# Two-layer decoder step: one row distance of 384 columns for all normed activations, other places for weights, staging tiles and slots

## The chip, the cores and the metric

The kernel runs on one core of a Trainium2 chip. The metric is the device time of one execution in microseconds. Three runs of the kernel before gave 2852.44, 2856.76 and 2860.83 us; the median is 2856.76. One more execution was taken by the hardware profiler and took 2856.44 us.

## The reference

One inference step of a decoder with two layers over T = 1104 tokens: 64 of eight sample requests, 16 meta tokens and 1024 of a prompt. The width is 1024, all values are fp32.

```python
for l in range(DEPTH):
    if l < N_A_LAYERS:
        a, (C, n, m) = mlstm_mixer(rmsnorm(h, norm_a), C0, n0, m0, lead, w_in_a, b_ig_a, b_fg_a, mh_norm_a, w_out_a)
        h = h + a
    else:
        h = h + fox_mixer(rmsnorm(h, norm_b), shared, attend, w_qo_b, q_norm_b, w_out_b)
    h = h + swiglu(rmsnorm(h, norm_ffn[l]), w_gate_up[l], w_down[l])
    if l == N_A_LAYERS - 1:
        shared = shared_kv(h, norm_kv, w_kvf, b_fg_b, k_norm_b)
y = rmsnorm(h, norm_final)
```

The first mixer is a gated linear recurrence. Its input and forget gates are what the change touches:

```python
li = softcap(gi + b_ig)                  # softcap(x) = 15 tanh(x / 15)
lf = log_sigmoid(softcap(gf + b_fg))
h, state = mlstm_sequence(q, k, v, li, lf, state0, lead)
out = (rmsnorm(h, mh_g) * sigmoid(og)) @ w_out
```

The second mixer is softmax attention with forget gates over keys and values that are projected once (`shared_kv`), for the samples also over cached pages.

## The kernel before

**Layout.** Activations lie with the features on the partitions: 8 rows of 128 features, and the tokens along a row. The tokens are cut in three slabs, of 336, 384 and 384 columns in phase A (the first mixer, `TSA`) and of 368 columns each in everything after it (`TS`). An fp32 product is made of three products of a fast 32-bit type: high by high, high by low, low by high (`mm3`, L269 to L274). So each weight and each normed activation is split in two tiles: ACT casts the high part (L334) and DVE takes the difference (L335). The normed activations are the tiles x0h, x0l, x1h, x1l, x2h, x2l of `new_x` (L354 and following), one pair for each slab, with 8 rows of n columns. Before the change a row begins right behind the one ahead of it, so that the distance from row to row is n columns: 336, 384 or 368.

**Two kinds of matmul read them.** In the token-major kind x is the stationary operand, 128 tokens of it, and 256 columns of weights move past it: the V, output gate and gate projections of phase A, and the K, V and q projections after the first layer (outputs named tmps). In the feature-major kind a block of weights is stationary and a whole slab of x moves: the q/k projections of phase A (mmA), the output projections (pops), the gate of the second mixer (bps) and gate/up in the feed-forward networks (L1540).

**Order.** TensorE (PE), the DMA queue of SyncE (SP) and part of DVE run in the order in which the code is written; the others are ordered by a scheduler, and the memory by pools: a tile that is put where another one was waits for the last use of that one. The stages by time, in microseconds from the start of the span: load and norm to 55; phase A with the recurrence 55 to 435; first output projection 444 to 545; first feed-forward to 1260; K, V and q projections to 1605; attention to 2020; second output projection to 2115; second feed-forward to 2850.

**The gates** (`rec_prep`, L964 and following). The biases are loaded on POOL's DMA queue into gbias (L970, L971), the start states into m (L973). DVE adds the bias (L1014), ACT takes the tanh (L1015), DVE scales (L1016) and copies the forget half (lf_tm, L1018), from which a chain on DVE and ACT makes the log of the sigmoid. PE transposes gates and then lf_tm (rps, L1030). Just ahead of this, `cache_prep` makes the running sums of the cached forget values: cs is stored to csE by eight DMAs of POOL (L959, 256 KB each) from the pool that lies where the rows' pool (`rp`) comes next. POOL also sets two selection tiles, selP and selS. Before the change gbias and m are in the pool of phase A (`kp`).

**First output projection** (in `mlp`, L510 and following). SP loads a block of 128 columns of w_out_a (L535) into a raw tile: woraw or one of two slots in turn; ACT and DVE split it into wo. The gate values ogc are loaded by POOL from ogD (L900), where phase A has stored them from staging tiles (stg, copied from PSUM by ACT at L859, stored by POOL at L860), and go through a sigmoid on ACT (L901). The last heads of the recurrence are gated and transposed (ghps, L1477) between the units of the projection (pops). Before the change woraw and wo lie where the staging tiles were.

**The rest that the change touches.** The slots are ten areas of the right side that hold weights in the output projections and feed-forwards. nq are tiles for the squares of the residual (L407 to L412), nr one for a norm. hr tiles of the hidden values of the feed-forward are put by `cut` over the memory of x (L1646).

Of the kernel before, what the change touches and what calls it, by code (L numbers as in the profile page):

```python
# [7 lines left out]
F32 = mybir.dt.float32  # L8
F32R = mybir.dt.float32r
# [24 lines left out]
TT = [(a + P * x, min(a + P * x + P, b)) for a, b in TS for x in range(3)]  # L34
WX = [max(z[t][1] - z[t][0] for z in (TSA, TS)) for t in range(3)]
GRPA = [(0, 1, 2, 3), (4, 5, 6), (7, 8)]
# [219 lines left out]
class Net:  # L256
# [98 lines left out]
    def new_x(self, t):  # L355

        ts = self.parts[0]
        n = ts[t][1] - ts[t][0]
        self.X[t] = tuple(
            self.xp.tile([P, KT * WX[t]], F32R, name=self.uid(f"x{t}{s}"), tag=f"x{t}{s}")[:, : KT * n].rearrange(  # L360
                "p (k n) -> p k n", k=KT) for s in "hl"
        )
        return self.X[t]
# [36 lines left out]
    def add_sq(self, H, t, m, sp, x, late=KT - 1):  # L400

        nc = self.nc
        t0, t1 = TS[t]
        n = t1 - t0
        if x == 0:
            self.sums[t] = self.ns[:, t % 2, :n]
            nc.scalar.activation(self.sums[t], H[t][:, m], AF.Square)  # L407
            return
        sq = self.nq[:, x % 2, :n]
        nc.scalar.activation(sq, H[t][:, m], AF.Square)  # L410
        s = self.sums[t]
        (nc.vector if x >= late else nc.gpsimd).tensor_tensor(out=s, in0=s, in1=sq, op=ALU.add)  # L412
# [35 lines left out]
    def run(self):  # L448
        nc, tc, I, O, ctx = self.nc, self.tc, self.I, self.O, self.ctx
        self.consts()  # L450
        self.hD = self.dram.tile([P, KT, T], F32, name="hD")
        self.X = {}
        self.parts = TSA, TTA
# [3 lines left out]
        with ExitStack() as c1:  # L457
# [16 lines left out]
            slots = {0: both[:, 0], 1: both[:, 1]}  # L474
            for x, n in ((7, NP), (3, NP), (8, NP + 104), (2, NP)):
                slots[x] = wp.tile([P, n], F32R, name=self.uid("slot"))
            ws = self.attend_prompt(ys, slots, both, I["w_out_b"][0])
# [5 lines left out]
    def mlp(self, H, w, l, heads=None, cb=None, early=None):  # L483
# [8 lines left out]
        with self.pool(self.uid("nsp")) as sp, self.pool(self.uid("npp"), bufs=2, space=PSUM) as pn:  # L492
# [3 lines left out]
            def small(c, down=False):  # L496
                p = c.enter_context(self.pool(self.uid("small")))
                if down:
                    self.nq = p.tile([P, 2, SL], F32, name=self.uid("nq"))
                    self.ny = lambda nm: p.tile([P, 2 * SL if l else max(2 * SL, 3 * 256)], F32, name=nm, tag="ny", bufs=3)  # L500
                    return p
                self.nq = p.tile([P, 2, SL], F32, name=self.uid("nq"))

# [3 lines left out]
            if cb:  # L507
                cw = cb
                wp = cw.enter_context(self.pool(self.uid("slots"), side="right"))
                slots = {x: wp.tile([P, self.wmin], F32 if x < 2 else F32R, name=self.uid("slot")) for x in range(10)}  # L510
            else:
# [4 lines left out]
            with ExitStack() as c:  # L516
                small(c)
                fixed.enter_context(self.tc.manual_schedule(engines={E.PE}))
                gp = c.enter_context(self.pool(self.uid("gh")))
                wp = c.enter_context(self.pool(self.uid("wo")))  # L520
                pp = c.enter_context(self.pool(self.uid("po"), bufs=3, space=PSUM))
# [99 lines left out]
            with cw if not cb else ExitStack():  # L621
                def each(t, m):
                    if cb or t < 2 or m < KT - 2:
                        self.add_sq(H, t, m, sp, m)
                    else:
                        n = TS[t][1] - TS[t][0]
                        nc.scalar.activation(self.nq[:, m % 2, :n], H[t][:, m], AF.Square)
                        if m == KT - 1:
                            nc.vector.tensor_tensor(out=self.sums[t], in0=self.sums[t], in1=self.nq[:, 0, :n],
                                                    op=ALU.add)  # L630
# [332 lines left out]
def rec_prep(self, kp, gates, rp, pp):  # L963
# [3 lines left out]
    if True:  # L967

        bias = kp.tile([P, 16], F32, name="gbias")
        nc.gpsimd.dma_start(bias[:, :8], I["b_ig_a"][0].partition_broadcast(P))  # L970
        nc.gpsimd.dma_start(bias[:, 8:], I["b_fg_a"][0].partition_broadcast(P))  # L971
        m0 = kp.tile([HA, NB], F32, name="m0")
        nc.gpsimd.dma_start(m0, I["state_m"][0].rearrange("b h -> h b"))  # L973
# [516 lines left out]
def ffn(self, H, flat, l, weights, order, mix, small, each, after, end, early=None):  # L1490
# [9 lines left out]
    with self.pool(f"ffn{l}") as fp, self.pool(f"ffnp{l}", space=PSUM) as pp:  # L1500
# [19 lines left out]
        class Unit:  # L1520
# [96 lines left out]
            def tail(u):  # L1617
# [11 lines left out]

        cut = lambda ts, n: [tuple(y.rearrange("p k n -> p (k n)")[:, i * 2 * SL : i * 2 * SL + 2 * SL] for y in ts)  # L1630
                             for i in range(n)]
# [16 lines left out]
        def h_split(j):  # L1648
            if j < len(hseq):
                t, z, c = seq[hseq[j]]  # L1650
                x0, x1, x2 = (cut(self.X[y], n) for y, n in ((0, 3), (1, 4), (2, 4)))
                a = [y for x in (2, 1, 4) for y in cut(Tx[x], 2)] + x2
# [245 lines left out]
def final(self, H, flat, t, gr, sp, pools):  # L1898
# [5 lines left out]
    r = sp.tile([P, 3], F32, name=self.uid("fr"), tag="fr", bufs=2)  # L1904
    squares = [self.sums[t]] + ([self.nq[:, 1, : TS[t][1] - s0]] if t == 2 else [])
    tiles = [(x, i, min(TT[i][0], TS[t][1] - P), TT[i][1]) for x, i in enumerate(GRP[t])]
# [588 lines left out]
def attend_prompt(self, ys, slots, both, w):  # L2495
# [3 lines left out]
    with self.pool("ap", bufs=1) as sp, self.pool("ap2", bufs=2) as s2, self.pool("app", bufs=2, space=PSUM) as pp:  # L2499
# [53 lines left out]
        def load_v(hp, e):  # L2553
# [6 lines left out]
            for g in QG:  # L2560
# [5 lines left out]

        more = {7: 72}
        row = lambda hp, qb, z: s2.tile([P, NM + P * qb + more.get(qb, 0)], F32, name=f"s{hp}_{qb}_{z}",
                                        tag=f"s{qb}")[:, : NM + P * qb]

# [303 lines left out]
```

## Time and profile before

| | us |
|---|---|
| three runs | 2852.44, 2856.76, 2860.83 |
| profiled execution | 2856.44 |
| its span | 2854.7 |
| PE, weight loads (PEld) busy | 2784.9, 2662.2 |
| DVE, ACT, POOL busy | 1747.1, 1318.4, 1079.4 |
| mean granted clock of TensorE | 0.995 |
| moved by DMA | 400.08 MB, 140 GB/s |

The page names instructions by line, engine, operation and tiles, `out<-in`. In rows of groups there stand the count, the busy time, the mean of one in ns and the idle time of the engine ahead of them with what ended it. A row of waits reads: engine, what waited, what it waited for, us in total, times, longest. A row of the timeline reads: start, us, engine, line, what, and in brackets the idle time before. A row of windows gives for a stretch its length and for each engine the busy time and the count, then the granted clock. In a row of DMA issues the last number is the median from issue to landing.

### The profile page before, as it was taken

To read this page: it belongs to the slowest core of one execution; us is meant where nothing else is said; L and a number is where in the kernel's file an instruction comes from. 1 tells how busy PE (TensorE), PEld (TensorE's weight loads), DVE (VectorE), ACT (ScalarE), POOL (GpSimd) and SP (SyncE) were. 2 spreads that over 40 slices of the span, in tenths; PEclk is the share of its full clock that TensorE was granted. 3 is DMA by queue.
4 is the path that set the end of the run, shared out by engine and by line. 5 is a ranking of instruction groups with operands and counts; after the bars stand their busy time and mean duration, and the time that the engine had idled before them with its cause. 6 is when DMAs were issued, how large, how long until landed. Compare 5 with 4: busy or idle time off the path is not lost. (4 is left out here: it accounts for less than half of the span.)

```text
span 2854.7 us, 54143 instructions
## 1 busy us (share of the span) xinstructions
PE 2784.9 (98%) x20638; PEld 2662.2 (93%) x20638; DVE 1747.1 (61%) x3598; ACT 1318.4 (46%) x2629; POOL 1079.4 (38%) x1578
## 2 busy tenths in 40 slices
PE   8999998999999999999999999999999999999999
PEld 7997988989999999999999888777999999999998
DVE  6144564787777755553365543777468777875553
ACT  6222464445444534443344554877444454443432
POOL 3042323166666411117463201455307566631110
PEclk9999999999999999999999999999999999999999
DMA  6157655222222275544453686452412222236653
GB/s 213 30 133 168 166 154 161 77 79 79 90 79 79 83 276 198 199 152 148 133 165 121 213 298 223 152 172 88 155 53 88 79 79 88 77 110 241 212 190 105
DMA packets 314070, 400.08 MB, mean 140 GB/s; under 512 B 28998, under 2 KB 235826, under 8 KB 312786
## 3 DMA queue, kind: packets, MB, share of 16 engines
q1 hardware_dynamic: 277282, 277.66, 30.6%
q0 software_dynamic: 35776, 118.40, 12.8%
q8 instruction: 162, 2.65, 0.4%
q10 hardware_dynamic: 752, 0.57, 0.1%
q14 instruction: 98, 0.80, 0.1%
HBM read 299.78 MB, written 96.77 MB: 139 GB/s over the span
## 5 line engine op out<-in xcount | busy, mean ns | idle before, releaser
L335 DVE TENSOR_TENSOR slot<-slot,slot 128x1024 fp32r<-128x1024 f32 (+3 forms) x263 | 251.6, 959 | 117.1 <-ACT slot L334 112.5
L334 ACT CAST slot<-slot 128x1024 fp32r<-128x1024 f32 (+3 forms) x263 | 206.6, 788 | 226.6 <-PE dps L273 100.2
L1540 PE MATMUL m<-x0h,slot 128*128 128x368 f32 x640 | 178.4, 329 | 0.0
L1540 PE MATMUL m<-x1h,slot 128*128 128x368 f32 x640 | 174.8, 332 | 3.6 <-DVE ns L1517 1.9
L412 POOL TENSOR_TENSOR ns<-ns,nq 128x368 f32<-128x368 f32 x59 | 65.2, 1104 | 213.5 <-ACT nq L410 212.3
L1646 POOL DMA_DIRECT2D hr<-hT x60 | 32.4, 541 | 283.8 <-DVE T_2l L335 70.6
L1540 PE MATMUL m<-x2h,slot 128*128 128x368 f32 x480 | 132.3, 330 | 0.0
L114 POOL TENSOR_TENSOR slot<-vA 128x256 f32<-128x256 f32 x80 | 74.3, 939 | 151.5 <-DMA vA<-in_w_gate_up 147.7
L114 POOL TENSOR_TENSOR slot<-Ht 128x256 f32<-128x256 f32 x80 | 74.6, 943 | 150.5 <-DMA Ht<-in_w_gate_up 78.8
L335 DVE TENSOR_TENSOR slot<-Ht,slot 128x256 fp32r<-128x256 f32 (+3 forms) x101 | 90.0, 892 | 53.0 <-ACT slot L334 53.0
L335 DVE TENSOR_TENSOR slot<-vA,slot 128x256 fp32r<-128x256 f32 (+3 forms) x101 | 88.8, 881 | 54.5 <-ACT slot L334 54.5
L1540 PEld LDWEIGHTS m<-x1h,slot 128*128 128x128 f32 x640 | 115.8, 188 | 6.5 <-DVE ns L1517 2.5
L1540 PEld LDWEIGHTS m<-x0h,slot 128*128 128x128 f32 x640 | 116.0, 188 | 0.0
L1540 PE MATMUL m<-x1l,slot 128*128 128x368 f32 x320 | 105.5, 330 | 0.0
L1540 PE MATMUL m<-x0l,slot 128*128 128x368 f32 x320 | 105.2, 329 | 0.0
L2668 ACT ACTIVATE s<-s,nb 128x272 f32<-128x272 f32 (+7 forms) x126 | 98.9, 787 | 0.3 <-POOL nb L2659 0.3
L2703 ACT COPY th<-tp 128x768 f32<-128x768 f32 (+1 forms) x80 | 73.6, 921 | 45.9 <-PE tp L2695 24.9
L1540 PE MATMUL m<-T_2h,slot 128*128 128x368 f32 x320 | 93.9, 334 | 0.0
L1540 PE MATMUL m<-T_4h,slot 128*128 128x368 f32 x320 | 92.7, 330 | 0.0
L335 DVE TENSOR_TENSOR slot<-wr,slot 128x1024 fp32r<-128x1024 f32 x42 | 54.3, 1293 | 60.5 <-ACT slot L334 60.5
L329 DVE SCALAR_TENSOR_TENSOR slot<-slot,gain,slot 128x256 fp32r<-128x256 f32 (+2 forms) x152 | 63.7, 467 | 43.7 <-ACT slot L328 42.9
L1540 PEld LDWEIGHTS m<-x2h,slot 128*128 128x128 f32 x480 | 86.8, 188 | 0.0
(857 smaller groups left out, 10352.1 us busy)
## 6 DMA issues: line engine op xcount, KB each, us to landing
slot<-in_w_down SPq DMA_DIRECT2D x88, 512.0 KB, 4.7
hr<-hT POOLq DMA_DIRECT2D x60, 368.0 KB, 5.3
wr<-in_w_down SPq DMA_DIRECT2D x42, 512.0 KB, 3.8
wraw<-in_w_in_a SPq DMA_DIRECT2D x40, 512.0 KB, 4.4
vA<-in_w_gate_up SPq DMA_DIRECT2D x40, 512.0 KB, 4.1
Ht<-in_w_gate_up SPq DMA_DIRECT2D x40, 512.0 KB, 4.0
kp<-in_cache_k SPq DMA_DIRECT2D x32, 512.0 KB, 6.0
vp<-in_cache_v SPq DMA_DIRECT2D x32, 512.0 KB, 8.3
```

Source lines behind the costliest of these rows:

```text
L114: self.net.nc.gpsimd.tensor_tensor(out=o, in0=a, in1=b, op=op)
L329: nc.vector.scalar_tensor_tensor(out=lo[:, k], in0=raw[:, k], scalar=gk, in1=hi[:, k].bitcast(F32), op0=ALU.mult, op1=ALU.subtract)
L334: self.nc.scalar.copy(hi, src)
L335: self.nc.vector.tensor_tensor(out=lo, in0=src, in1=hi.bitcast(F32), op=ALU.subtract)
L412: (nc.vector if x >= late else nc.gpsimd).tensor_tensor(out=s, in0=s, in1=sq, op=ALU.add)
L1540: nc.tensor.matmul(u.b[b][:, :SL], w[p][:, k], x[q][:, k], start=new and k == i == 0, stop=k == 1 and i == 2, skip_group_check=True)
L1646: nc.gpsimd.dma_start(hraw[j], hT[t][:, 2 * c : 2 * c + 2])
L2668: nc.scalar.activation(ss[z, u], ss[z, u], AF.Exp, bias=nb[:, z : z + 1], accum_out=sm[:, u, z : z + 1])
L2703: nc.scalar.copy(th.rearrange("p x z (u h q) -> p h (x z u) q", h=2, q=64)[:, :, :n], pt[:, :, :n])
```

## The change

1. The x tiles have a row distance of 384 columns (1536 bytes) throughout. `flat_x` keeps the whole tiles, from which `cut` takes its pieces. Casts, differences and other work of DVE and ACT on two rows of x at 368 columns are then 128x2x368 where they were 128x736; the count of instructions is the same, and PE's order of matmuls and SP's order of loads are too.
2. gbias and m0 move from the pool of phase A to the pool of the rows.
3. In the first output projection a tile "rest" of 4 x 368 columns, which nothing uses, lies at the start of the gate tiles' pool. It moves the pool of weights (woraw, wo) 6912 bytes up, behind the staging tiles; the gate tiles ogc now lie on staging tiles.
4. Slots other than 0, 1, 2, 3, 7 and 8 have 1024 columns, not 1088, slot 8 of the second mixer loses 104 columns, and a padding of a row in the prompt's attention goes.
5. In the last down projection there is one tile nq, and nr serves as the second.

```diff
-        self.X[t] = tuple(
-            self.xp.tile([P, KT * WX[t]], F32R, name=self.uid(f"x{t}{s}"), tag=f"x{t}{s}")[:, : KT * n].rearrange(
-                "p (k n) -> p k n", k=KT) for s in "hl"
-        )
+        self.flat_x[t] = [self.xp.tile([P, KT * SLA], F32R, name=self.uid(f"x{t}{s}"), tag=f"x{t}{s}") for s in "hl"]
+        self.X[t] = tuple(x.rearrange("p (k n) -> p k n", k=KT)[:, :, :n] for x in self.flat_x[t])
...
-        sq = self.nq[:, x % 2, :n]
+        sq = self.nq(x % 2)
...
-            for x, n in ((7, NP), (3, NP), (8, NP + 104), (2, NP)):
-                slots[x] = wp.tile([P, n], F32R, name=self.uid("slot"))
+            for x in (7, 3, 8, 2):
+                slots[x] = wp.tile([P, NP], F32R, name=self.uid("slot"))
...
-                    self.nq = p.tile([P, 2, SL], F32, name=self.uid("nq"))
+                    nq = p.tile([P, 1 if l else 2, SL], F32, name=self.uid("nq"))
+                    self.nq = lambda x: self.nr if l and x else nq[:, x]
...
-                slots = {x: wp.tile([P, self.wmin], F32 if x < 2 else F32R, name=self.uid("slot")) for x in range(10)}
+                slots = {x: wp.tile([P, self.wmin if x in (0, 1, 2, 3, *LOW[:2]) else KT * P], F32 if x < 2 else F32R,
+                                    name=self.uid("slot")) for x in range(10)}
...
                 gp = c.enter_context(self.pool(self.uid("gh")))
+                if heads:
+                    gp.tile([P, 4 * SL], F32, name="rest")
                 wp = c.enter_context(self.pool(self.uid("wo")))
...
-        bias = kp.tile([P, 16], F32, name="gbias")
+        bias = rp.tile([P, 16], F32, name="gbias")
...
-        m0 = kp.tile([HA, NB], F32, name="m0")
+        m0 = rp.tile([HA, NB], F32, name="m0")
...
-                x0, x1, x2 = (cut(self.X[y], n) for y, n in ((0, 3), (1, 4), (2, 4)))
+                x0, x1, x2 = (cut(self.flat_x[y], n) for y, n in ((0, 3), (1, 4), (2, 4)))
```

The loads of the biases move on POOL. Its order at the start of the program before (grows are the gains of the norms, cap and bm masks, m the start states):

```order
L706 DMA grows<-in_mh_norm_a 8x128
L970 DMA gbias<-in_b_ig_a 128x8
L971 DMA gbias<-in_b_fg_a 128x8
L973 DMA m_1875<-in_state_m 8x8x1
L990 MEMSET cap 128x128
```

and now, at the place where the running sums cs are stored and the selection tiles are set:

```order
L835 DMA qkD<-stg_2050 128x384
L960 DMA csE<-cs 128x512 x8
L971 DMA gbias<-in_b_ig_a 128x8
L972 DMA gbias<-in_b_fg_a 128x8
L974 DMA m_1875<-in_state_m 8x8x1
L976 MEMSET selP 8x512
L983 MEMSET selS 64x512
```

The three loads have moved behind the eight stores of cs, and lie in memory that the tiles of the running sums held before.

On DVE the work that needs the biases moves with them. Before, the add and the scaling stood much earlier, between two splits of weights (wlo), and at the place of the rows there was only this (rs and stk are rows that are set to constants, lse the start of the chain for the log of the sigmoid):

```order
L956 SCALAR_TENSOR_TENSOR cs<-cso,csl 128x512
L957 COPY clast<-cs 128x1
L1018 COPY lf_tm<-gates 128x72
L1034 MEMSET rs 8x1104
L342 SCALAR_TENSOR_TENSOR lse_1958<-lf_tm 128x72
L1035 MEMSET rs 8x8
L1036 MEMSET rs 8x1
L1037 MEMSET rs 8x8
L1046 MEMSET stk 104x1104
L344 TENSOR_SCALAR lsz_1959<-lse_1958 128x72
```

Now the same place on DVE reads:

```order
L957 SCALAR_TENSOR_TENSOR cs<-cso,csl 128x512
L958 COPY clast<-cs 128x1
L1035 MEMSET rs 8x1104
L1047 MEMSET stk 104x1104
L1036 MEMSET rs 8x8
L1037 MEMSET rs 8x1
L1038 MEMSET rs 8x8
L1015 TENSOR_TENSOR gates<-gates,gbias 128x144
L1017 TENSOR_SCALAR gates<-gates 128x144
L1019 COPY lf_tm<-gates 128x72
L341 SCALAR_TENSOR_TENSOR lse_1958<-lf_tm 128x72
L343 TENSOR_SCALAR lsz_1959<-lse_1958 128x72
```

The add and the scaling have come down to it, and the setting of rs and stk stands ahead of them. PE's transposes of gates keep their place in PE's order.

At the start of the first output projection it is ACT's order that differs. Before (stg are the last staging copies, woraw and slot the raw weights, ogc the gate values):

```order
L859 COPY stg_4847<-mmA_4746 128x384
L859 COPY stg_4875<-mmA_4850 128x384
L901 ACT_TABLE_LOAD
L901 ACTIVATE ogc_4996<-ogc_4996 128x272
L901 ACTIVATE ogc_4999<-ogc_4999 128x272
L901 ACTIVATE ogc_5009<-ogc_5009 128x272
L334 CAST wo_353_4929<-woraw_4927 128x1024
L334 CAST wo_354_4933<-slot_4900 128x1024
L334 CAST wo_355_4940<-slot_4901 128x1024
L334 CAST wo_357_4948<-woraw_4946 128x1024
```

and now:

```order
L860 COPY stg_4847<-mmA_4746 128x384
L860 COPY stg_4875<-mmA_4850 128x384
L333 CAST wo_353_4930<-woraw_4928 128x1024
L902 ACT_TABLE_LOAD
L902 ACTIVATE ogc_4997<-ogc_4997 128x272
L333 CAST wo_354_4934<-slot_4900 128x1024
L333 CAST wo_355_4941<-slot_4901 128x1024
L902 ACTIVATE ogc_5000<-ogc_5000 128x272
L902 ACTIVATE ogc_5010<-ogc_5010 128x272
L333 CAST wo_357_4949<-woraw_4947 128x1024
```

The first cast of weights has come ahead of the table load and the gates, the next two ahead of two of the gates. The loads of all three ogc on POOL, whose order hardly changes, now wait for stores of staging tiles, since they write where those tiles were; before, only the third did.

More of the change, by code (lines that the diff above doesn't have):

```diff
@@ L34 @@
 TT = [(a + P * x, min(a + P * x + P, b)) for a, b in TS for x in range(3)]
-WX = [max(z[t][1] - z[t][0] for z in (TSA, TS)) for t in range(3)]
 GRPA = [(0, 1, 2, 3), (4, 5, 6), (7, 8)]
@@ L451, in run @@
         self.hD = self.dram.tile([P, KT, T], F32, name="hD")
-        self.X = {}
+        self.X, self.flat_x = {}, {}
         self.parts = TSA, TTA
@@ L498, in small @@
                 if down:
-                    self.nq = p.tile([P, 2, SL], F32, name=self.uid("nq"))
+                    nq = p.tile([P, 1 if l else 2, SL], F32, name=self.uid("nq"))
+                    self.nq = lambda x: self.nr if l and x else nq[:, x]
                     self.ny = lambda nm: p.tile([P, 2 * SL if l else max(2 * SL, 3 * 256)], F32, name=nm, tag="ny", bufs=3)
                     return p
-                self.nq = p.tile([P, 2, SL], F32, name=self.uid("nq"))
+                nq = p.tile([P, 2, SL], F32, name=self.uid("nq"))
+                self.nq = lambda x: nq[:, x]
             if cb:
@@ L625, in each @@
                     else:
-                        n = TS[t][1] - TS[t][0]
-                        nc.scalar.activation(self.nq[:, m % 2, :n], H[t][:, m], AF.Square)
+                        nc.scalar.activation(self.nq(m % 2), H[t][:, m], AF.Square)
                         if m == KT - 1:
-                            nc.vector.tensor_tensor(out=self.sums[t], in0=self.sums[t], in1=self.nq[:, 0, :n],
+                            nc.vector.tensor_tensor(out=self.sums[t], in0=self.sums[t], in1=self.nq(0),
                                                     op=ALU.add)
@@ L1627, in tail @@
                 yield
-        cut = lambda ts, n: [tuple(y.rearrange("p k n -> p (k n)")[:, i * 2 * SL : i * 2 * SL + 2 * SL] for y in ts)
+        cut = lambda ts, n: [tuple((y if len(y.shape) < 3 else y.rearrange("p k n -> p (k n)"))[:, i * 2 * SL : i * 2 * SL + 2 * SL] for y in ts)
                              for i in range(n)]
@@ L1904, in final @@
     r = sp.tile([P, 3], F32, name=self.uid("fr"), tag="fr", bufs=2)
-    squares = [self.sums[t]] + ([self.nq[:, 1, : TS[t][1] - s0]] if t == 2 else [])
+    squares = [self.sums[t]] + ([self.nq(1)] if t == 2 else [])
     tiles = [(x, i, min(TT[i][0], TS[t][1] - P), TT[i][1]) for x, i in enumerate(GRP[t])]
@@ L2565, in attend_prompt @@
         vals = {}
-        more = {7: 72}
-        row = lambda hp, qb, z: s2.tile([P, NM + P * qb + more.get(qb, 0)], F32, name=f"s{hp}_{qb}_{z}",
-                                        tag=f"s{qb}")[:, : NM + P * qb]
+        row = lambda hp, qb, z: s2.tile([P, NM + P * qb], F32, name=f"s{hp}_{qb}_{z}", tag=f"s{qb}")
         first, firstc, firsts = {}, {}, {}
```

## The prediction

> **What bounds the kernel now.** I read the page's busy times first, then the waits of TensorE, then stretches of the span.
>
> ```profile
> span 2854.7 us, 54143 instructions
> PE 2784.9 (98%) x20638; PEld 2662.2 (93%) x20638; DVE 1747.1 (61%) x3598; ACT 1318.4 (46%) x2629; POOL 1079.4 (38%) x1578
> ```
>
> TensorE (PE) is busy 98% of the span, and no other engine passes 61%. So only two kinds of edit count: one that changes how long a matmul takes, and one that adds or removes a wait of PE. Everything else lies under the 2784.9 us. The waits of PE that lie near the change:
>
> ```profile
> PE pops L272 <- ACT wo L334: 9.0, 1, 9.0
> PE rps L1030 <- ACT csl L954: 1.4, 1, 1.4
> PE mmA L272 <- ACT stg L833: 1.4, 1, 1.4
> PE rps L1030 <- ACT whi L334: 0.9, 1, 0.9
> ```
>
> The first is the longest idle stretch of PE in the whole run, at the start of the first output projection.
>
> **Part 1: gbias and m0 move to the pool of the rows.** Their loads go behind the eight stores csE<-cs on POOL's queue. Before, POOL issued them at the start; the stores come much later:
>
> ```profile
> 4.74 0.58 POOL L970 DMA_DIRECT2D gbias<-in_b_ig_a  x1
> 5.31 0.55 POOL L971 DMA_DIRECT2D gbias<-in_b_fg_a  x1
> 140.92 4.25 POOL L959 DMA_DIRECT2D csE<-cs  x8 [1.47 <-DVE clast L957]
> 149.94 0.52 POOL L982 MEMSET selS<- 64x512 f32 x1 [4.26 <-DMA csE<-cs]
> ogD<-stg POOLq DMA_DIRECT2D x16, 192.0 KB, 2.6
> ```
>
> POOL has issued the eight stores at 140.92 + 4.25 = 145.17, so the biases are issued no earlier than 145.2 and 145.7. They stand behind 2 MB of stores on the same queue, and the last of those had landed at 149.94, when POOL's next instruction was released. The last row above is the time to landing of another small transfer of that queue. Here are the consumers, and, in the last row, what the two bias loads took to land at the start of the run:
>
> ```profile
> 139.17 0.78 PE L1030 MATMUL rps<-ident,gates 80*8 80x80 f32 x6 [1.40 <-ACT csl L954]
> L1014 DVE TENSOR_TENSOR gates<-gates,gbias x1: 305/305/305, 56.9 to 56.9; 128x144 f32<-128x144 f32 x1
> L1016 DVE TENSOR_SCALAR gates<-gates x1: 235/235/235, 57.6 to 57.6; 128x144 f32<-128x144 f32 x1
> DMA to landing us min/median/max: 6.1/6.3/6.5
> ```
>
> PE comes to the transposes of gates at 139.17 and, as it runs in order, everything behind them waits too: 48 matmuls mmA, then the transposes of lf_tm. From the start of the add to the end of the scaling it took 57.6 + 0.235 − 56.9 = 0.95 us. To it come some 0.15 us from the scaling to PE, an estimate from the 0.2 or so between neighbours in these rows. Earliest landing: the biases pass the stores and take the 2.6 us of ogD<-stg, 148.3, so PE starts at 149.4: +10.2. Latest: 6.3 us after 145.7, 152.0, PE at 153.1: +13.9. I take a landing one microsecond after the stores are through, 150.9, PE at 152.0, **+12.8**. The bound is nearer the late end since two loads of 32-byte rows follow a full queue.
>
> A stall that long costs more behind it, as the end of the 9 us one shows:
>
> ```profile
> core 0: us, PE busy (x) PEld busy (x) DVE busy (x) ACT busy (x) POOL busy (x), PEclk, DMA share, GB/s
> 443.88:447.90 4.02, 3.74 (x11) 3.26 (x12) 3.15 (x3) 2.09 (x2) 0.00 (x0) 0.50 0.79 212
> 447.90:452.00 4.10, 4.10 (x28) 4.07 (x27) 3.82 (x4) 1.33 (x2) 0.00 (x0) 1.00 0.58 162
> ```
>
> After it PE ran 4.0 us at a granted clock of 0.50 and did about half the work: +2.0. Two waits then go: the 0.9 before the transposes of lf_tm (DVE's memsets now stand ahead of the chain, not inside it), and the 1.4 of mmA for stg, since ACT and POOL catch up while PE stands. What was hidden under PE, POOL's selects among it, stays hidden: they end about 1 us later than before while PE is 12 later. Sum of part 1: 12.8 + 2.0 − 0.9 − 1.4 = **+12.5** (10 to 14).
>
> The Trainium skill ("DMA: Bandwidth & Descriptors", Queues, rings and completion order) says that each DMA engine takes descriptors of one ring in order, and (SWDGE vs HWDGE vs iDMA) that only one queue serves POOL's DMAs; by it the early end falls away, and the third rival's 2844 with it, while the sum stays. The 4.26 us for which POOL waited on these stores fits that, and no run here yet shows a small load behind them.
>
> **Part 2: the first output projection.** The raw weights no longer lie where the staging tiles were, and the gate tiles ogc now do.
>
> ```profile
> SPq L535 <- DMA ogD<-stg: 32.3, 2, 31.7
> 438.52 0.37 SPq L535 DMA_DIRECT2D woraw<-in_w_out_a  x1
> 442.78 1.04 ACT L334 CAST wo<-woraw 128x1024 fp32r<-128x1024 f32 x1 [1.98 <-DMA woraw<-in_w_out_a]
> 443.86 1.22 DVE L335 TENSOR_TENSOR wo<-woraw,wo 128x1024 fp32r<-128x1024 f32 x1 [9.40 <-ACT wo L334]
> 435.40 1.28 ACT L901 ACT_TABLE_LOAD   x1
> 437.91 0.54 POOL L900 DMA_DIRECT2D ogc<-ogD  x1 [1.63 <-DMA ogD<-stg]
> 440.37 0.43 ACT L901 ACTIVATE ogc<-ogc 128x272 f32<-128x272 f32 x1 [2.81 <-DMA ogc<-ogD]
> 447.20 3.77 SPq L535 DMA_DIRECT2D slot<-in_w_out_a  x2
> 451.72 1.05 ACT L334 CAST slot<-slot 128x1024 fp32r<-128x1024 f32 x1 [1.58 <-DMA slot<-in_w_out_a]
> ```
>
> The loads of weights waited 31.7 us for the staging stores. Now they don't, and the raw weights are there when ACT is through with its last copy of staging at 435.40, so the first cast (1.04) ends at 436.45. PE's first product starts there rather than at 443.88: −7.4. But all three ogc loads now wait for the last staging store, as the third did (437.91), and ACT holds them between the first and the second cast: ogc lands at 440.4, the table load (1.28) and the gate (0.43) end at 442.1, the second cast at 443.1, its low part on DVE (1.22) at 444.3. The reload of that slot follows then, not at 447.20, so 2.9 earlier; and on that reload hangs the cast of 451.72 and what follows it, the next heads' transposes. So PE starts 7.4 earlier and waits most of it again before the second and third tile. Ends: 0 (the chain of reloads takes it all) and −7.4. I take the chain: **−2.5**, a little under its 2.9, for handovers.
>
> **Part 3: the row distance, x as the weights.** In phase A the tiles x1 and x2 already have 384 columns to a row and x0 has 336; in the K, V and q projections after the first layer all have 368.
>
> ```profile
> L272 PE MATMUL tmps<-whi,x1h 128*128 128x256 f32 x72 | 19.9, 276 | 0.0
> L274 PE MATMUL tmps<-whi,x0l 128*128 128x256 f32 x48 | 13.5, 281 | 0.0
> L273 PE MATMUL tmps<-slot,x1h 128*128 128x256 f32 x176 | 49.3, 280 | 0.0
> L272 PE MATMUL tmps<-slot,x0h 128*112 128x256 f32 x88 | 24.6, 279 | 0.0
> 107.00:127.00 20.00, 20.00 (x177) 20.00 (x176) 0.00 (x0) 2.84 (x8) 0.00 (x0) 1.00 0.00 1
> ```
>
> The same product of 256 columns takes 276 ns with a distance of 384 (one started each 20.00/177 = 113.0 ns) and about 280 with 336 or 368. Only the distance differs in phase A between the first two rows. Nine groups of 176 and nine of 88 make 2376 such matmuls later, with some 400 of 272 columns and of x0: 2376 × 4 ns = −9.5, with the others **−10**. PE has no idle time in those stretches, so all of it counts. Ends: 0 (the distance isn't the reason) and −14 (5 ns on 2,800).
>
> **Part 4: x as the moving operand.** Three rows, the timeline for 336 and 384 columns (whose groups have 23 and 23 steps) and a stretch of 368:
>
> ```profile
> 140.62 0.31 PE L273 MATMUL mmA<-x0l,whi 128*128 128x336 f32 x1
> 144.17 0.34 PE L272 MATMUL mmA<-x1h,whi 128*128 128x384 f32 x1
> 148.16 0.34 PE L274 MATMUL mmA<-x1h,wlo 128*128 128x384 f32 x1
> 640.00:980.00 340.00, 340.00 (x2028) 337.83 (x2027) 268.32 (x424) 163.17 (x336) 211.35 (x204) 1.00 0.26 83
> L1540 PE MATMUL m<-x0h,slot 128*128 128x368 f32 x640 | 178.4, 329 | 0.0
> L1540 PE MATMUL m<-x2l,slot 128*128 128x368 f32 x240 | 79.0, 329 | 0.0
> L272 PE MATMUL pops<-x0h,wo 128*128 128x368 f32 x64 | 22.2, 347 | 9.0 <-ACT wo L334 9.0
> L273 PE MATMUL bps<-x0l,slot 128*128 128x368 f32 x48 | 15.8, 329 | 0.0
> ```
>
> 336 columns: 3.55/23 = 154.3 ns; 384 at a distance of 384: 3.99/23 = 173.5; 368 at 368: 340/2028 = 167.7. Scaled by columns, 173.5 × 368/384 = 166.2 (−1.5); by the slope between the first and the second, 173.5 − 16 × 0.40 = 167.1 (−0.6). The matmuls with x moving are 2640 in the feed-forward (six groups), 1152 in the two output projections and 480 in the last query and gate projections: about 4,300. I take −1.2 ns: **−5** (0 to −6.5). The smaller slots shift where weights start; no row separates that, so I price it at nothing, with ±4 in the range.
>
> **The rest.** Casts and differences in two pieces of 368 rather than 736, and one square buffer for two in the last layer, fall on DVE and ACT (61% and 46%) under a busy PE: 0, up to +2 where PE waits for DVE at the start of a feed-forward or at the end.
>
> **Sum**: +12.5 − 2.5 − 10 − 5 = −5.0. Against the profiled run's own 2856.44 (2854.7 in the span and 1.7 around it) that is 2851.4; the median of the runs, 2856.76, stands 0.3 above it. I forecast **2851 us**.
>
> **Rivals.**
> - **The distance does nothing.** Where 336 and 368 only look dearer than 384 for another reason, parts 3 and 4 are nil and the late biases stand alone: 2856.4 + 12.5 − 2.5 = 2866. The place is PE's transposes of gates, the price 12.5, and it decides from the point at which parts 3 and 4 give less than some 1.5 us together (the sum is then above 2865). Against it: 276 beside 281 ns for one shape in one stretch; for it: these differ by less than 2%, and the ends of matmuls are modelled. The Trainium skill ("TensorE: Matmul & The Clock Gate", Back-to-back issue gap) gives a start-to-start time that depends on the columns alone, so it speaks for this rival and its 2866; the two rows at equal columns speak against it.
> - **The moving operand gains as much as the weights.** 4 ns on 4,300 matmuls is −17 in place of −5: 2839. For it: both kinds read the same rows of x; against it: 173.5 at 384 columns beside 154.3 at 336 leaves little room.
> - **The stall is shorter and the output projection keeps its 7.4.** Biases that pass the stores make part 1 10.2 + 2.0 − 0.9 − 1.4 = +9.9, and with −7.4 in place of −2.5 the time is 2844. For it: nothing shows a small load behind stores; against it: the loads at the start took 6.3 us.
>
> **How the numbers follow.** The forecast as it stands: 0.55, its own range 2845 to 2857, of which 0.22 lies below 2848. A strong effect on the moving operand 0.16, short stall with full gain 0.15, no effect 0.14. About 0.3% (8.6 us) is what a measurement can tell from no change, so faster means below 2848 and slower above 2865. Faster: 0.22 + 0.15 + 0.10 = 0.47, the two last from the second and third rival with a little left over; slower: 0.11 of the first rival's 0.14; the rest, 0.42, is within 0.3%. The range takes in the slots' ±4 below the second rival and the first rival's own time: 2834 to 2866.
>
> **What would show it.** The transposes rps<-gates of PE released by DVE's scaling near 152 us rather than 139; a PE clock of 0.5 for some 4 us behind; the first pops near 436.5 with 4 to 5 us of new waits before the third tile; 276 rather than 280 ns for tmps<-slot; L1540 near 329 still, and a few more than 2028 matmuls in 340 us. Wrong would be a stall under 8 us, an unchanged 280, or waits of PE in the feed-forward that grow by more than 2 us.

## The result and the profile after

The changed kernel takes 2873.39 us (median of five runs, 2872.77 to 2876.00) beside 2856.76 for the kernel before: a ratio of 1.0061 with a 95% interval from 1.0047 to 1.0076. It is 0.6% slower, the other way from the forecast and above its range (2834 to 2866). Its profiled execution took 2876.00 us, the slowest of the five, so a comparison of the two traces shows 19.6 us where the medians show 16.6.

The page after: busy times of the engines. Then the waits of TensorE (PE) in the changed kernel that differ most from those of before, longest first (us in total, times, longest), and below them a wait of before:

```profile
span 2874.3 us, 54148 instructions
PE 2786.1 (97%) x20638; PEld 2662.6 (93%) x20638; DVE 1742.2 (61%) x3598; ACT 1317.1 (46%) x2629; POOL 1074.1 (37%) x1578
```

```profile
PE rps L1031 <- DVE gates L1017: 13.1, 1, 13.1
...
PE nps L1352 <- issue: 6.3, 1, 6.3
PE pops L271 <- ACT wo L333: 5.5, 2, 4.0
...
PE sp L2635 <- DMA slot<-qDl: 4.5, 1, 4.5
...
PE sp L2635 <- DMA slot<-kDh: 2.3, 1, 2.3
...
PE sp L2635 <- DMA slot<-kDl: 1.6, 1, 1.6
```

```profile
PE sp L2636 <- DMA slot<-qDl: 0.8, 1, 0.8
```

PE is busy 2786.1 us, 1.2 more than before; so 18.4 of the 19.6 us are idle time, and the busy time shows no gain of the size forecast for the matmuls. Two of these places were in the forecast, the gates (rps) and the output projection (pops). A third was not: the first scores of the prompt attention (sp) wait for the loads of q and k, 8.4 us in all, where before they waited 0.8. The wait of nps, in the recurrence, was 3.8 before.

Since PE runs the same matmuls in the same order in every version, one can subtract: how much later than in the kernel before does the same matmul start? This table is worked out from the starts in the traces. Stretches are named by the time in the trace of before. A column is one profiled execution: of the changed kernel (after) and of the experiments e1 to e11, which are told below. The first stretch, with the same work in all of them, shows that entries of about 1 us can be chance; at the start of the prompt attention e5, e6 and e7 do the same work too and differ by up to 3.8 us.

| stretch (us) | what | after | e1 | e2 | e3 | e4 | e5 | e6 | e7 | e8 | e9 | e10 | e11 |
|---|---|---|---|---|---|---|---|---|---|---|---|---|---|
| 0–138 | load, first projections | −1.2 | −1.6 | −0.6 | −0.5 | −1.1 | −1.0 | −0.5 | −0.8 | −0.4 | −1.5 | −1.5 | −0.5 |
| 138–220 | gates | 9.1 | 11.8 | 2.2 | 2.3 | −1.5 | 1.5 | 2.2 | 0.3 | 1.8 | 8.1 | 8.4 | 2.1 |
| 220–444 | recurrence | 1.4 | −1.7 | −0.4 | 0.9 | −0.8 | −3.2 | 0.5 | 1.5 | −1.9 | 0.2 | 0.7 | −1.5 |
| 444–520 | output projection, start | 0.9 | −0.6 | 1.7 | 0.2 | 0.3 | −0.1 | 0.3 | −4.0 | −3.3 | 3.9 | 0.8 | −3.6 |
| 520–1262 | rest of it, feed-forward | −0.3 | −0.4 | 0.6 | 0.8 | 0.2 | 0.7 | 0.6 | 0.3 | 0.7 | 1.0 | 0.6 | 0.0 |
| 1262–1610 | K, V, q projections | −1.5 | −1.6 | −1.9 | −1.6 | 0.0 | −1.6 | −1.8 | −1.8 | −7.4 | −1.9 | −0.1 | −7.5 |
| 1610–1765 | sample attention | 0.7 | 0.0 | 1.3 | 1.5 | 1.6 | 1.4 | 1.5 | 0.4 | 1.6 | 1.7 | 3.0 | 0.1 |
| 1765–1860 | prompt attention, start | 11.9 | 8.3 | 12.9 | 9.6 | 9.9 | 9.2 | 6.3 | 5.4 | 5.8 | 0.4 | −0.1 | 1.8 |
| 1860–2560 | rest of it, feed-forward | 0.4 | 0.1 | 0.4 | −0.3 | 0.1 | 0.2 | 0.6 | 0.7 | 1.1 | 0.2 | 0.4 | 0.3 |
| 2560–2846 | last down projection | −1.5 | −1.5 | −1.5 | −1.5 | 0.0 | −1.1 | −1.1 | −1.0 | −1.1 | −1.5 | 0.0 | −1.5 |

Now the gates. The timeline of the changed kernel on POOL and PE:

```profile
143.58 0.55 POOL L971 DMA_DIRECT2D gbias<-in_b_ig_a  x1
144.12 0.55 POOL L972 DMA_DIRECT2D gbias<-in_b_fg_a  x1
144.66 0.63 POOL L974 DMA_DIRECT2D m<-in_state_m  x1
147.56 0.51 POOL L976 MEMSET selP<- 8x512 f32 x1 [2.27 <-DMA csE<-cs]
```

```profile
149.26 2.04 PE L1031 MATMUL rps<-ident,gates 80*8 80x80 f32 x9 [13.09 <-DVE gates L1017]
150.96 0.63 PE L271 MATMUL mmA<-x0h,whi 128*128 128x336 f32 x1
151.38 0.48 PE L272 MATMUL mmA<-x0l,whi 128*128 128x336 f32 x1
151.66 0.47 PE L273 MATMUL mmA<-x0h,wlo 128*128 128x336 f32 x1
151.94 0.35 PE L271 MATMUL mmA<-x0h,whi 128*128 128x336 f32 x1
```

PE stands 13.09 us for the biases (DVE's gates, which waited for them), and its first matmuls behind take half as long again (0.48 against 0.32 later on), for some 3 us until 151.9. The windows view gives the clock there (length, busy time and count of each engine, PEclk, DMA share, GB/s):

```profile
149.00:152.00 3.00, 2.74 (x13) 1.94 (x14) 2.37 (x9) 1.53 (x4) 2.63 (x14) 0.50 0.00 0
443.00:450.00 7.00, 4.83 (x27) 4.21 (x26) 1.60 (x3) 1.70 (x3) 2.74 (x6) 1.00 0.92 263
```

The second of these rows is the start of the output projection. There the DMA engines are now 0.92 busy (0.45 before, from 434 to 441), and the timeline shows what that does to the gate values ogc, on POOL and on ACT:

```profile
444.62 0.55 POOL L861 DMA_DIRECT2D ogD<-stg  x1 [0.45 <-ACT stg L860]
448.93 1.60 POOL L901 DMA_DIRECT2D ogc<-ogD  x3 [3.76 <-DMA ogD<-stg]
```

```profile
444.23 1.05 ACT L333 CAST wo<-woraw 128x1024 fp32r<-128x1024 f32 x1
452.43 1.28 ACT L902 ACT_TABLE_LOAD   x1 [7.16 <-DMA ogc<-ogD]
453.73 0.43 ACT L902 ACTIVATE ogc<-ogc 128x272 f32<-128x272 f32 x1
454.06 1.98 ACT L333 CAST wo<-slot 128x1024 fp32r<-128x1024 f32 x2
```

The first cast and PE's first product come as early as forecast. But POOL waits 3.76 us for the staging stores (1.63 before), and the first gate values land 8.1 us after the start of the first cast, where 5.0 were forecast; so the second cast is at 454.06, 9.8 us after the first, and PE waits for it.

Last, the prompt's loads. SP's timeline before and after:

```profile
1754.92 0.43 SPq L2550 DMA_DIRECT2D slot<-qDh  x1
1755.40 0.43 SPq L2550 DMA_DIRECT2D slot<-kDh  x1
1755.87 0.43 SPq L2550 DMA_DIRECT2D slot<-kDl  x1
1756.35 0.43 SPq L2549 DMA_DIRECT2D slot<-cD  x1
1770.28 0.32 SPq L2550 DMA_DIRECT2D slot<-qDl  x1
```

```profile
1779.06 0.34 SPq L2551 DMA_DIRECT2D slot<-qDh  x1
1779.45 0.42 SPq L2551 DMA_DIRECT2D slot<-kDh  x1
1779.92 0.42 SPq L2551 DMA_DIRECT2D slot<-kDl  x1
1780.39 0.43 SPq L2550 DMA_DIRECT2D slot<-cD  x1
1780.86 0.62 SPq L2551 DMA_DIRECT2D slot<-qDl  x1
```

The queue's own waits name the reason, before and after:

```profile
SPq L2550 <- PE bps L274: 13.4, 1, 13.4
```

```profile
SPq L2551 <- PE bps L273: 15.3, 1, 15.3
```

The wait is hardly longer, but it has moved. Before, four of the five went out early and only qDl waited for the last matmul of the gate projection (bps), which reads slot 8. Now qDh, the first in the queue, waits for it, and four others stand behind. The sizes in the code tell why. Both groups of slots end at the same byte. Before, slot 9 took 1088 columns, 4352 bytes, at the end, and slot 8 ended below them; the tile of qDh takes the last 1040 columns, 4160 bytes, so 192 bytes lay between. Slot 9 at 1024 columns moves slot 8 up by 256 bytes: it now reaches 64 bytes into the tile of qDh, and the program lets a tile wait for another one whole.

### The profile page after: what moved, and what is told of

The parts are those of the page before. It is cut to its first block, busy times and chain, and to the rows that moved or that the text cites. A ratio compares the mean times of both kernels' runs of the same rounds, so it can differ in the third digit from the quotient of the medians.

```text
span 2874.3 us, 54148 instructions
## 1 busy us (share of the span) xinstructions
PE 2786.1 (97%) x20638; PEld 2662.6 (93%) x20638; DVE 1742.2 (61%) x3598; ACT 1317.1 (46%) x2629; POOL 1074.1 (37%) x1578
## 5 line engine op out<-in xcount | busy, mean ns | idle before, releaser
L113 POOL TENSOR_TENSOR slot<-vA 128x256 f32<-128x256 f32 x80 | 75.6, 955 | 151.9 <-DMA vA<-in_w_gate_up 78.0
L409 POOL TENSOR_TENSOR ns<-ns,nq 128x368 f32<-128x368 f32 x50 | 54.1, 1083 | 178.8 <-ACT nq L407 178.1
```

Of the source, the lines that this page charges most:

```text
L113: self.net.nc.gpsimd.tensor_tensor(out=o, in0=a, in1=b, op=op)
```

## The experiments

Theory after the result, of three independent things: the late biases cost some 10 us, the prompt loads held by the overlap of slots some 11 us, and the row distance does next to nothing. The rival: the row distance itself costs time, in memory or in transfers, and undoing the two leaves the kernel slow.

**e1: slot 9 back to 1088 columns.**

```diff
-                slots = {x: wp.tile([P, self.wmin if x in (0, 1, 2, 3, *LOW[:2]) else KT * P], F32 if x < 2 else F32R,
+                slots = {x: wp.tile([P, self.wmin if x in (0, 1, 2, 3, 9, *LOW[:2]) else KT * P], F32 if x < 2 else F32R,
```

> The changed kernel with slot 9 at 1088 columns again (256 bytes more), nothing else undone. Slot 8 then ends at 224992 bytes of the partition as before, 192 bytes below the tile of the first prompt load (qDh at 225184), where in the changed kernel it ended at 225248 and overlapped it by 64 bytes. Theory (the overlap holds the whole queue of prompt loads behind the last bps matmul): the loads of qDh, kDh, kDl and cD are issued some 15 us ahead of qDl again, PE's waits of sp for qDl, kDh and kDl (4.5 + 2.3 + 1.6 us) go, with the half clock behind them: 11 us below the changed kernel's 2873.4, 2862. Rival (the loads are late because DMA is busy or because another wait takes the place): 2870 or more, with the waits of sp still above 5 us.

Measured: 2871.56 us, ratio to before 1.0064 (1.0050 to 1.0078). The edit gave nearly nothing, 1.8 us by the medians. The loads show why:

```profile
1760.54 0.42 SPq L2551 DMA_DIRECT2D slot<-qDh  x1
1761.01 0.43 SPq L2551 DMA_DIRECT2D slot<-kDh  x1
1775.89 0.32 SPq L2551 DMA_DIRECT2D slot<-kDl  x1
1776.25 0.43 SPq L2550 DMA_DIRECT2D slot<-cD  x1
1776.73 0.43 SPq L2551 DMA_DIRECT2D slot<-qDl  x1
```

Two loads are early again and three still late: slot 8 now overlaps the tile of kDl by 384 bytes. The change had also taken 104 columns from the prompt's slot 8, the tile of qDl, and these were what had kept the tile of kDl below slot 8. So neither padding is enough alone; I had looked at one only.

**e2: gbias back in the pool of phase A** (the start states m stay with the rows).

```diff
-        bias = rp.tile([P, 16], F32, name="gbias")
+        bias = kp.tile([P, 16], F32, name="gbias")
```

> The changed kernel with gbias back in the pool of phase A; the start states m stay with the rows. Theory (the late biases alone make the stall at the gates): the transposes of gates no longer wait 13.1 us, some 1.4 us of other waits come back there, the granted clock stays at 1.00: 10 to 11 us below the changed kernel, 2863. Rival (the chain behind is late for another reason, the start states or the selection tiles, that the stall only covers): the stall moves to a later wait of PE in 150 to 240 us, 2868 or more.

Measured: 2867.66 us, 1.0038 (1.0024 to 1.0052). In the table the stretch of the gates falls from +9.1 to +2.2: the 13.1 us are gone, and a wait of mmA for stg, 1.4 before, is 3.3. The medians show 5.7 of the 10 expected, with runs of e2 from 2861.45 to 2871.05, wider than those of the change.

**e3: both.**

> Both of the former edits: the changed kernel with gbias in the pool of phase A and slot 9 at 1088 columns. What is left of the change is the row distance, the place of the weights and gate tiles in the first output projection, the other slots and the square buffers. Theory (the two waits are all that made it slower, and they are independent): the two gains add up, 2852, some 4 us below the kernel before, from the stretches in which matmuls got a little shorter. Rival (the row distance costs time elsewhere): 2857 or more. My forecast of the row distance (15 us gained) would give 2842.

Measured: 2864.16 us, 1.0029 (1.0017 to 1.0040): above the 2852 expected. The time alone would fit the rival (2857 or more); the trace speaks against it, since the excess stands in one place, the prompt's stretch, which still has its +9.6.

**e4: the kernel before with slot 9 at 1024 columns.**

```diff
-                slots = {x: wp.tile([P, self.wmin], F32 if x < 2 else F32R, name=self.uid("slot")) for x in range(10)}
+                slots = {x: wp.tile([P, KT * P if x == 9 else self.wmin], F32 if x < 2 else F32R, name=self.uid("slot")) for x in range(10)}
```

> The kernel before with one edit: slot 9 at 1024 columns rather than 1088, so that slot 8 moves up by 256 bytes and overlaps the tile of the first prompt load by 64 bytes. Theory: the prompt loads wait for the last bps matmul, PE waits some 8 us for them and runs at half clock behind: 2867, 10 to 11 above the kernel before. Rival (the wait needs the other slot sizes or the row distance too): 2857.

Measured: 2865.08 us, 1.0037 (1.0023 to 1.0051). One slot that is 256 bytes smaller makes the kernel before 10 us slower, all of it at one place, +9.9 between 1765 and 1860. PE's waits there are those of the change:

```profile
PE sp L2636 <- DMA slot<-qDl: 4.3, 1, 4.3
PE sp L2636 <- DMA slot<-kDh: 2.4, 1, 2.4
PE sp L2636 <- DMA slot<-kDl: 1.5, 1, 1.5
```

So the third loss of the change comes from the place of the slots, not from the row distance.

**e5: as e3, with slot 8 lying below the tile of cD alone.**

```diff
-            both = wp.tile([P, 2, NP], F32, name="slot01")
-            slots = {0: both[:, 0], 1: both[:, 1]}
-            for x in (7, 3, 8, 2):
-                slots[x] = wp.tile([P, NP], F32R, name=self.uid("slot"))
+            slots = {x: wp.tile([P, NP], F32R, name=self.uid("slot")) for x in (7, 3, 8)}
+            both = wp.tile([P, 2, NP], F32, name="slot01")
+            slots[2] = wp.tile([P, NP], F32R, name=self.uid("slot"))
+            slots.update({0: both[:, 0], 1: both[:, 1]})
```

> As e3 (gbias in the pool of phase A, slot 9 at 1088 columns), and the tiles of the prompt loads are put in another order: kDh, kDl, qDl, then the tile of cD, then qDh. Slot 8, which the last bps matmul reads, then lies wholly below the tile of cD, so that of the loads only cD and qDl behind it wait for it. In e1 and e3 slot 8 still overlapped the tile of kDl by 384 bytes, since the 104 columns that the change took from the prompt's slot 8 had kept the two apart. Theory (any small load behind that wait is late): PE's wait of sp for qDl and kDl goes from 6 us to under 2, the stretch from 1765 to 1860 us comes back from +9.6 to within 2 us of the kernel before, 2855. Rival (the wait comes from the transfers themselves, which got slower): 2863.

Measured: 2862.61 us, 1.0029 (1.0016 to 1.0041). The expectation missed: +9.2 in the profiled execution (6.3, 5.4 and 5.8 in e6, e7 and e8, which keep this order of the tiles). PE waits in one piece:

```profile
PE sp L2635 <- DMA slot<-qDl: 5.0, 1, 5.0
```

cD is 1040 KB, qDl 520, and cD stands ahead of qDl in the queue. Before, cD went out 14 us ahead of qDl; now the two go out together, at 1767.54 and 1767.90. That qDl lands late because cD is ahead of it is argued, not shown; e9 shows that the wait goes when neither is held. So few loads that wait are no help if the largest is among them.

**e6: e5 without the unused tile "rest".**

> As e5, without the unused tile in the pool of the gate tiles, so the weights of the first output projection lie on the staging tiles again, and the gate tiles don't. Theory (PE starts 7.4 us earlier there and waits it all again for the gate tiles and the reload): the stretch from 444 to 520 us within 1 us of e5, the 9 us wait of pops in one piece as in the kernel before; total equal to e5 within 2 us. My forecast of that part gives e5 a gain of 2.5: 2.5 above e5.

Measured: 2864.65 us, 1.0029 (1.0018 to 1.0041). In the stretch 444 to 520 e5 stands at −0.1 and e6 at +0.3. So the new place of the weights gave nothing there; the medians, 2.0 apart with runs that overlap, don't tell more.

**e7: e5 with "rest" behind the gate tiles.**

```diff
-                    gp.tile([P, 4 * SL], F32, name="rest")
+                    c.enter_context(self.pool(self.uid("rest"))).tile([P, 4 * SL], F32, name="rest")
```

> As e5, with the unused tile in a pool of its own behind the gate tiles: the weights of the first output projection lie behind the staging tiles as in the change, but the gate tiles lie where they were before, not on staging tiles, and two of three are loaded early. Theory (the gate tiles' loads behind the staging stores are what gave the 7.4 us back): PE's waits from 434 to 520 us fall from 12 to some 6 us, 4 to 6 below e5: 2850. Rival (the reload of slots behind the second low part takes it back in any case): equal to e5 within 1.5.

Measured: 2858.16 us, 1.0014 (1.0005 to 1.0023), 4.4 below e5, and −4.0 in the stretch (−3.3 and −3.6 in e8 and e11, which keep the edit). PE's waits there are one of 4.5 us (9.0 before):

```profile
PE pops L271 <- ACT wo L333: 4.5, 1, 4.5
PE pops L273 <- DVE wo L334: 0.3, 1, 0.3
```

The gain that the change looked for is there, once the gate tiles do not lie on staging tiles.

**e8: e7 with the third token tile 128 columns wide** (in the K, V and q projections; the 16 output rows more are read by nobody).

```diff
+        if ts is TS and i % 3 == 2:
+            return tuple(x.rearrange("p (k n) -> p k n", k=KT)[:, k, a : a + P] for x in self.flat_x[t])
...
+        if self.parts[0] is TS:
+            for x in self.flat_x[t]:
+                nc.gpsimd.memset(x.bitcast(F32).rearrange("p (k n) -> p k n", k=KT)[:, :, n:], 0.0)
...
-                self.mm3(ps[:m, :n], xh, xl, wh[:, k % 4, :], wl[:, k % 4, :], k == 0, k == KT - 1)
+                self.mm3(ps[: xh.shape[1], :n], xh, xl, wh[:, k % 4, :], wl[:, k % 4, :], k == 0, k == KT - 1)
```

> As e7, and the third token tile of each slab in the K, V and q projections is read 128 columns wide, not 112: the 16 columns behind it, free at a row distance of 384, are set to zero by POOL and their 16 output rows are read by nobody. In the trace of the change these matmuls start each 120 ns where the stationary tile is 112 wide and each 114 ns where it is 128 wide, all with the same start within 512 bytes. Theory (the width of the stationary tile sets the difference): 792 matmuls by 6 ns, 5 us below e7, 2845; phase B's windows at 114 ns. Rival (the place of the third tile sets it): equal to e7.

Measured: 2853.44 us, 0.9993 (0.9984 to 1.0002), 4.7 below e7; −5.6 more in the projections' stretch (−7.4 against −1.8). The groups by shape, one row of the kernel before, then of the change, then of e8 (count | busy us, mean ns of one | idle):

```profile
L273 PE MATMUL tmps<-slot,x1h 128*112 128x256 f32 x88 | 24.7, 281 | 0.0
```

```profile
L272 PE MATMUL tmps<-slot,x1h 128*128 128x256 f32 x176 | 48.9, 278 | 0.0
...
L272 PE MATMUL tmps<-slot,x1h 128*112 128x256 f32 x88 | 24.9, 283 | 0.0
...
L272 PE MATMUL tmps<-wlo,x0h 128*128 128x256 f32 x48 | 13.6, 283 | 0.0
```

```profile
L272 PE MATMUL tmps<-slot,x1h 128*128 128x256 f32 x264 | 73.0, 276 | 0.0
```

In the change the 128 wide tiles of this group took 278 ns (280 before), but the 112 wide ones went up from 281 to 283. With all three tiles at 128 wide the group stands at 276. So at a distance of 384 the forecast's 4 ns came only when the third tile was full too. Full tiles at the old distance of 368 were not tried, so how much of this is the distance and how much the width alone stays open.

**e9: the change with the slots in another order.**

```diff
-                                    name=self.uid("slot")) for x in range(10)}
+                                    name=self.uid("slot")) for x in (8, 3, 0, 1, 2, 4, 5, 6, 7, 9)}
```

> The changed kernel with one edit: the ten slots are placed in the order 8, 3, 0, 1, 2, 4, 5, 6, 7, 9, with the sizes of the change, so that slots 8 and 3, which the last bps matmuls read, lie below all tiles that the prompt loads fill. No prompt load then waits for bps. In e5 the tile of cD still did, and qDl behind it in the queue: PE waited 5.3 us for qDl. Theory (the wait of the prompt loads for the last slots is the whole loss there): the stretch 1765 to 1860 us within 1.5 us of the kernel before (+11.9 in the change), 10 to 12 below the change: 2862. Rival (the loads run into another wait or into the attention's own transfers): 2868 or more.

Measured: 2863.68 us, 1.0027 (1.0015 to 1.0038), 9.7 below the change. The start of the prompt attention stands at +0.4, and the waits for loads are gone from it:

```profile
PE sp L2635 <- DVE mx L2644: 2.8, 6, 0.9
PE op L2731 <- ACT th L2702: 0.8, 1, 0.8
```

The sizes are those of the change and nothing else is edited, so this settles the third loss. The one odd entry is +3.9 at the output projection, in a single execution.

**e10: the kernel before with gbias and m in the rows' pool.**

> The kernel before with gbias and m moved to the pool of the rows, nothing else. Theory: PE waits some 13 us for the gates and runs at half clock for a while behind; 2 to 3 us come back in the recurrence, where PE waited for others before: +9 to +10, 2865. Rival (the recurrence absorbs it, or the whole 12.5 of my forecast stays): 2860, or 2868.

Measured: 2867.96 us, 1.0045 (1.0031 to 1.0059), 13 above before by the medians. The trace gives +8.4 at the gates and +0.7 in the recurrence, and PE's wait is that of the change:

```profile
PE rps L1030 <- DVE gates L1016: 13.1, 1, 13.1
PE rps L1030 <- ACT lf L1032: 1.0, 1, 1.0
```

The stall needs nothing but the place of the biases. The medians show 4 us more; in the profiled execution there is a further +3.0 in the sample attention, where PE waits 2.0 us for a load of cached keys (0.2 before). The edit doesn't touch that place, and whether this is chance was not tried.

**e11: all that helped** (e8 with e9's order of slots in place of e5's order of the prompt's tiles, and slot 9 at 1024).

> As e8, with the slots in the order of e9 in place of the other order of the prompt's tiles, and slot 9 at 1024 columns as in the change: the changed kernel with early biases, the gate tiles where they were, third token tiles 128 wide, and no prompt load behind bps. Theory: e8 less the 5.8 us of the stretch 1765 to 1860: 2848, 7 below the kernel before, by 5 us of matmuls in the K, V and q projections, 3 in the first output projection, 1 in the last down projection, less 2 in the recurrence. Rival (a new wait in the feed-forward, whose slots lie elsewhere now): 2853.

Measured: 2845.80 us, 0.9972 (0.9959 to 0.9984): 8.7 below the kernel before beside it, and faster than both kernels.

## Why the prediction was wrong

Two terms of the sum failed. The smaller slots were priced at nothing and cost 11.9 us in the trace; that put the time outside the range. The row distance was priced at −15 in parts 3 and 4 and gave about −1.5; that turned the sign. e9 shows the two apart: without the loss at the slots the change takes 2863.68 us, within the range, but still 9.2 above the kernel beside it (2854.50).

**Part 1, the late biases: right in mechanism, size near.** The stall came at the place and from the releaser that were named. It is 13.1 us of idle time; the forecast's 12.8 is how much later the transposes start, and that was 11.7, as PE had waited 1.4 there before. The loads landed 4.0 to 4.4 us after issue, at about 148.3, behind the last of the stores (147.56). Half clock lasted 3 us rather than 4. Up to 220 us, 9.1 were left. Of the two waits that were to go, the 1.4 for stg went; the 0.9 ahead of lf_tm went too, but one of 1.0 for lf came in its place. Some 1.7 us came back by the clock, which the forecast did not have: from 180 to 200 us the granted clock was 0.91, in the same matmuls before (170 to 190) 0.83. In the recurrence the wait of nps grew from 3.8 to 6.3 (5.4 in e10). So the whole was +10.5 up to 444 us (+9.1 in e10), where 12.5 were forecast.

**Part 2, the first output projection: the chain was right, its prices were not.** The step "ogc lands at 440.4" took the landing times of before, when no block of w_out_a was loaded beside the staging stores. The edit itself starts those loads; with the DMA engines 0.92 busy POOL waited 3.76 us for the stores rather than 1.63, and the −2.5 became −0.6 to +1.7 in after, e1, e2, e3 and e5 (+3.9 in e9; +0.3 in e6, without the edit). That the gate tiles on staging tiles are what loses it, e7 shows: −4.0.

**Part 3, x as the weights: a step that failed.** "Only the distance differs in phase A between the first two rows" is wrong. The tiles of x0 in phase A start at columns 0, 80 and 208, those of x1 at 0, 128 and 256. After the change x0 has the distance of 384 as well, and its 128 wide tiles still take 283 ns. So the distance alone was not the reason for 281 against 276 there, and what it gave later was −1.5 us in place of −10: −2 ns on the full tiles, and +2 to +4 on the 112 wide ones. With full tiles throughout (e8) the stretch gives −7.4, which is most of the forecast. What in the start or width of a tile sets the time is not settled; e8 changes the width alone.

**Part 4, x as the moving operand: nothing.** Here is the same length of the feed-forward after, by the windows view:

```profile
640.00:980.00 340.00, 340.00 (x2029) 338.79 (x2029) 266.73 (x426) 163.38 (x336) 212.07 (x205) 1.00 0.26 81
```

2029 matmuls beside 2028 is 0.1 ns each, where 1.2 were forecast, and the two long feed-forward stretches of the table stand at −0.3 and +0.4. The scaling from three rows of different widths was finer than the rows could bear. The last down projection gained 1.5 us, which I had not forecast and which e4 and e10 (without the rest of the change) don't show; which part of the change gives it was not tried.

**The smaller slots, "nothing, with ±4": the step that failed most, +11.9.** I priced them by where weights start for a matmul and did not ask which later tile each slot shares memory with. The order of the instructions did not move at all there, so it could not show; what moved was one wait, from the fifth of five loads to the first. Putting slot 8 out of reach gives it back (e9), and moving it into reach makes the kernel before 10 us slower (e4).

**The rivals.** The first, "the distance does nothing", with 2866, was the nearest: its place was there, and its price nearly. The time lies 7 above it. That it is no further off is partly luck: the loads of the prompt cost 11.9 that it didn't have, the output projection did not give its 2.5, and against that the biases cost 2 less, and the K, V and q projections and the last down projection each gave back 1.5. The second and third rival didn't happen: the moving operand gained nothing, and the biases did not pass the stores. (The second rival's 2839 less the slots' 4 is 2835, not the 2834 of the range; this changes nothing.) The rule of the Trainium skill that descriptors of one ring are taken in order ("DMA: Bandwidth & Descriptors", Queues, rings and completion order) fits the loads at 148.3 behind stores that were through by 147.56. The start-to-start time by columns alone that the Trainium skill gives ("TensorE: Matmul & The Clock Gate", Back-to-back issue gap) does not fit the K, V and q projections of the changed kernel, where one shape of moving operand goes at 114 ns from start to start with a 128 wide tile and at 120 with a 112 wide one (medians, worked out from the starts in the trace). On the row distance it was still the better guide: the gain was 1.5 us, not 15.

## What to carry to other kernels

When an edit changes sizes in a memory that is used again, list for each tile that moved what it now overlaps and which instruction that makes wait; a wait that goes to the head of an in-order queue takes all behind it along, and 64 bytes were enough. Where an edit lets transfers start earlier, take the landing times of the others from a moment at which the queues are as busy as they will be then. And before a difference between two rows is put down to one property, look for a row that has that property and not the others.

## What the runs showed of the hardware

With 256 moving columns the mean time of a matmul differed with the stationary tile. In phase A of the changed kernel it was 276 ns at 128 wide and starts at 0, 128 and 256 columns, and 283 at 128 wide and starts at 80 and 208. In the K, V and q projections, whose tiles start at 0, 128 and 256, it was 283 for the 112 wide third tile and 277 to 284 for the full ones beside it; with the third tile full too (e8) it was 276 to 282. Two loads of 32-byte rows behind 2 MB of stores on POOL's queue landed 4.0 to 4.4 us after issue, less than the 6.1 to 6.5 that the same two took at the start of the kernel before. Behind a stall of 13.1 us PE ran some 3 us at a granted clock of 0.50.
